# How far instructions may run ahead, set for each stage, and 24 columns of layer 1's first expert table in whole fp32

## The chip, the cores and the metric

The kernel runs on one core of a Trainium2 chip. The metric is the time of one execution on the device in microseconds (us), the median over several executions. PE is TensorE (matrix products), DVE VectorE, ACT ScalarE, POOL GpSimd, SP SyncE, which here issues most of the DMAs.

## The reference

Two layers of a diffusion block over 256 latent rows `x` and 256 context rows `ctx`, each 1024 wide. Each layer has a token mixer (differential attention, windowed attention and a gated delta rule, merged by gates) and a feed-forward part that looks up experts:

```python
def peer_ffn(h, wq, keys, u_tab, v_tab):            # cut
    q = (t @ wq).reshape(n, PEER_HEADS, 2, PEER_HALF)          # 8 heads
    s = jnp.einsum('thcd,cnd->thcn', q, keys)                  # 2 x 128 keys
    sv, si = lax.top_k(s, PEER_TOPK)                           # 16 of 128
    ...
    cv, ci = lax.top_k(cand, PEER_TOPK)                        # 16 of 256 sums
    eid = (i1 * N_KEYS + i2).reshape(n, PEER_HEADS * PEER_TOPK)
    gw = jax.nn.softmax(cv, axis=-1)
    act = gelu(einsum('pd,ped->pe', tb, u_tab[eb]))
    return einsum('pe,ped->pd', act * gb, v_tab[eb])

for l in range(DEPTH):                               # DEPTH = 2
    ...
    m, mc = token_mixer(h, hc, ...)                  # mc only in layer 0
    x = x + gt1 * m
    x = x + gt2 * peer_ffn(modulate(x, ...), ...)
    if need_ctx:                                     # layer 0
        xc = xc + gt1c * mc
        xc = xc + gt2c * peer_ffn(modulate(xc, ...), ...)
```

All of it is fp32. The output is `x` after layer 1.

## The kernel before

**Stages.** In order of the program: the context mixer of layer 0, the context's route of experts, the latent mixer of layer 0, the dense expert part of layer 0, the context mixer of layer 1, the latent mixer of layer 1, the dense expert part of layer 1. The context's experts of layer 0 are done in another way than the latent ones: `peer_gather` fetches the rows that were chosen out of both tables (U0, V0 for one half of the 256 rows, U1, V1 for the other) with indirect DMAs, one DVE instruction ("gather dot") for each fetched row of the first table, and small PE products for the second. This work is a lane of its own that runs beside the latent mixer and the dense part of layer 0, and its sum `acc` is stored to memory and read again by `add_peer` at the start of layer 1.

**The dense part** (`peer_dense`) multiplies all 16384 experts: the first table is taken as 128 columns of 128 experts (`first`, label "dU"), then Gelu, then the product with the weights of the route, then the second table (label "dV"). A column of the first table is 512 KB. It is multiplied in one of two ways. *Split:* ACT rounds the column to fp32r (the high part), DVE subtracts that from the column (the low part), and `mm3` multiplies high by high, high by low and low by high: 3 x 8 products of 128x256. *Whole:* 8 products in fp32 of the column and a third copy `full` of the normed rows that `norm_T` then keeps. In layer 0 columns 0 to 31 (`U4`) are whole, in layer 1 none. The route (`route`, eight heads, each: projection with `wq` split by DVE and ACT, scores, top 16 twice) and the building of the weight tables (`weights`, labels "didx" and "build") have a higher priority (`RBASE`) than the columns, which fill gaps; `pre` columns (32 in layer 0, 64 in layer 1) may be multiplied ahead of the second table.

**The order.** No engine's order is written by hand. `Rec.add` records every operation, and `Rec.order` plans all of them as a list scheduler with costs of its own; it gives out tiles of four sizes (`b4`, `b2`, `b1` in SBUF, `ps` in PSUM). An operation that takes a new tile out of the program's order is asked for its distance: the work, in us of the planner's own costs, between it and the first operation of its lane that isn't planned yet. `blocked` refuses it beyond `FAR` = 80; beyond `NEAR` = 20 it must leave some tiles of each size free (`SPARE`). One exception: in the context mixer of layer 1 (`FREE1`), once the gather lane is done, there is no limit to the distance, with other numbers of tiles left free (`FREE`). All instructions of the program are issued from one line of `emit` (L627 before, L624 after), so the profile's rows are told apart by tiles and shapes: `b` is any working tile, `ps` PSUM, `rows` and `ga` the gather's, `psv`, `pcd`, `pii`, `pgw` the route's.

Of the kernel before, what the change touches and what calls it, by code (L numbers as in the profile page):

```python
# [39 lines left out]
NC = sum(ni * nj for _, ni, nj in CAND)  # L40
LEVELS = (1, 2, 4, 8, 16, 32, 64)
WN = 32
U4, V4 = range(32), ()
WPOOL = ()
UP0, UP1 = (), ()
PRE1 = 64
# [5 lines left out]

ACTB = (1, 1)
GBASE, RBASE = 0, -8000
TAIL, FREE1 = 0, True
FREE = {"b4": 4, "b2": 2, "b1": 1, "ps": 0}
PRE = 32
LOAD = {"tensor": 1.0, "vector": 0.3, "scalar": 0.2}
NEAR, FAR, URGENT = 20.0, 80.0, 0.0

WHOLE = range(16)
LOADS = 0
# [207 lines left out]

class Op:
    __slots__ = ("i", "eng", "meth", "args", "kw", "dur", "dma", "preds", "succ", "tiles", "prio",
                 "npred", "ready", "lab", "lane", "cw", "port", "free")


NAMES = []
# [10 lines left out]
class Rec:  # L287
# [5 lines left out]
    def __init__(self, nc, pools, bufs):  # L293
        self.nc, self.pools, self.bufs = nc, pools, bufs
        self.ops, self.tiles = [], []
        self.tensor, self.vector = Eng(self, "tensor"), Eng(self, "vector")
        self.scalar, self.gpsimd, self.sync = Eng(self, "scalar"), Eng(self, "gpsimd"), Eng(self, "sync")
        self.base = 0
        self.lane, self.cw, self.free = 0, {}, False
        self.lab = ""  # L300
        self.why, self.prevt, self.inslot, self.fin = {}, {}, {}, {}

# [46 lines left out]
    def add(self, eng, meth, args, kw):  # L349
        o = Op()  # L350
# [34 lines left out]
                    t.acc = [a for a in t.acc if not ((a[3] | reg) == reg and pr[0] <= a[2][0] and a[2][1] <= pr[1])]  # L385
            t.acc.append((o.i, wr, pr, reg))
        o.preds = list(preds)
        o.lane, o.free = self.lane, self.free
        o.cw = self.cw[o.lane] = self.cw.get(o.lane, 0.0) + o.dur * LOAD.get(eng, 0.0) * (URGENT if self.base == RBASE else 1.0)
        o.prio = self.base + o.i  # L390
        o.succ = []
# [12 lines left out]
    def order(self):  # L404
# [89 lines left out]
        def blocked(o):  # L494
            for t in o.tiles:
                if t.kind == "dr" or t in live:
                    continue
                if not slots[t.tag] and not borrow(t.tag):
                    return t.tag
                f = first[t]  # L500
                lane = owner[t.tag]
                front = ops_at(lane)
                if f > front:
                    keep = 0
                    if o.lane >= 0:
                        head = ops[lanes[o.lane][lpos[o.lane]]]
                        dist = o.cw - head.cw
                        free = o.free and lpos[-1] >= len(lanes[-1]) - TAIL
                        if dist > FAR and not free:
                            return "far"  # L510
                        if free and dist > NEAR:
                            keep = FREE.get(t.tag, 0)
                        elif dist > NEAR or o.lane != main:
                            keep = SPARE.get(t.tag, 0) + (LOADS if o.dma and t.tag == "b4" else 0)
                    if load[t.tag][front:f].max() + 1 > cap[t.tag] - keep:
                        return t.tag
            return None
# [113 lines left out]
class Kern:  # L631
# [1138 lines left out]
        return newS, self.out_proj(mT, xt, l, pr, s)  # L1770

    def run(self):
        self.setup()
        self.silu_c()
        pr, pr1 = self.layer_cols(0), self.layer_cols(1)
        self.layer_rows(0, pr)
        self.ada(0, pr, 0, 8)
        kv = self.kv_tiles()
        hT = self.norm1(self.I["ctx"], pr, 1)
        fill = [lambda n=n: self.ada(1, pr1, n, n + 1, 2) for n in range(24)]  # L1780
        if ADA1 == 3:
            self.fill = fill
        S, oTs = self.main(0, 1, hT, pr, kv, None, True)
        self.ada(0, pr, 8, 24)
        mT = self.merge(hT, 0, pr, oTs)
        xc, xs = self.out_proj(mT, self.I["ctx"], 0, pr, 1)
        self.dump("xc0", xc)
        F = self.peer_front(0, 1, xs, pr)
        self.wpool = WPOOL
        if ADA1 == 4:  # L1790
            self.fill = fill
        self.whole = True
        _, (x, xs) = self.mix(0, 0, self.I["x"], pr, kv, S)
        self.whole = False
        self.dump("x0", x)
        self.layer_rows(1, pr1)
        self.nc.lane, self.nc.base = -1, GBASE
        acc = self.peer_gather(0, 1, F)
        self.nc.lane, self.nc.base = 0, 0

        def extra(c0):
            if ADA1 == 2 and c0 % 4 == 0 and c0 >= 32:
                self.ada(1, pr1, c0 // 4 - 8, c0 // 4 - 7, 2)
        x = self.peer_dense(0, 0, x, xs, pr, u4=U4, v4=V4, extra=extra, pre=PRE, up=UP0)
        self.dump("x1", x)
        self.wpool = ()
        pass
        self.lab("1 norm1")
        self.nc.free = FREE1
        xs = self.add_peer(1, xc, acc, pr)  # L1810
        hT = self.norm_T(xs, pr1["A1"][:, :, 1], pr1["mod"][:, 0:8, 1])
        kv = self.kv_tiles()
        S, _ = self.main(1, 1, hT, pr1, kv, None, False)
        self.nc.free = False
        _, (x, xs) = self.mix(1, 0, x, pr1, kv, S)
        self.dump("x2", x)
        self.peer_dense(1, 0, x, xs, pr1, self.out, pre=PRE1, up=UP1)


def body(tc, I, out, dbg=None):  # L1820
# [22 lines left out]
```

## Time and profile before

| | |
|---|---|
| median of three runs | 3811.16 us (3800.89 to 3819.09) |
| the profiled execution, its own time | 3817.58 us |
| its span in the profile | 3815.8 us |
| PE busy | 3463.5 us |
| DVE, ACT, POOL busy | 2374.0, 1707.0, 818.8 us |
| layer 1's dense part | 2866 to 3813 us |

The span is the time between the first and the last recorded instruction. Busy times are shares of that span; times of single instructions are given from its start.

### The profile page before, as it was taken

What the parts mean: (1) busy time and instruction counts of PE and PEld (TensorE: products, weight loads), DVE (VectorE), ACT (ScalarE), POOL (GpSimd) and SP (SyncE); (2) the same over time, 40 slices, a digit from 0 to 9 for tenths busy, and PEclk for the clock granted to TensorE, in tenths of its full rate; (3) what the DMA queues carried; (4) which work ended last, traced back from release to release, by engine and by line L of the source; (5) the groups of instructions that cost most, each with busy time, mean ns of one, the idle gap of its engine ahead of it and who ended that gap; (6) DMA issues with size and microseconds to landing.
All of it is one profiled execution on the core that took longest, in us unless ns stands there. A gap on an engine that the chain in (4) does not pass through costs nothing.

```text
span 3815.8 us, 62556 instructions
## 1 busy us (share of the span) xinstructions
PE 3463.5 (91%) x23800; PEld 2960.3 (78%) x23800; DVE 2374.0 (62%) x5288; ACT 1707.0 (45%) x3554; POOL 818.8 (21%) x716
## 2 busy tenths in 40 slices
PE   8999994987998987999999999998995789999999
PEld 6875993876797674788777778887795679889998
DVE  4542569887556783988544455645568963665554
ACT  4743441541543181343333347763543564444443
POOL 1010001476123434655444311101010000000000
PEclk9996997988899998999999998989997899999999
DMA  6346753597277889999899961212262364776562
GB/s 256 117 138 223 239 191 127 181 332 274 75 254 276 292 291 394 409 372 365 337 359 338 342 250 40 84 45 94 62 233 72 119 185 150 243 280 227 199 211 105
DMA packets 300956, 837.67 MB, mean 220 GB/s; under 512 B 26736, under 2 KB 96752, under 8 KB 300656
## 3 DMA queue, kind: packets, MB, share of 16 engines
q1 hardware_dynamic: 153168, 522.80, 38.6%
q0 software_dynamic: 73728, 268.47, 18.9%
q10 hardware_dynamic: 73760, 42.40, 3.7%
q8 instruction: 188, 3.08, 0.3%
q14 instruction: 112, 0.92, 0.1%
HBM read 792.67 MB, written 40.89 MB: 218 GB/s over the span
## 4 chain that ended last, share of the span: by engine, by line
PE 49%; DVE 4%; ACT 3%; issue 1%; DMA 1%; ACTq 0%; POOL 0%; POOLq 0%; DVEq 0%
PE ps L627 49%; ACT b L627 3%; DVE b L627 3%; DVE psi L627 0%; DVE psv L627 0%; ACTq L627 0%; DMA gd<-b 0%; DMA b<-in_v_tab 0%; DMA b<-in_u_cols 0%; DVE pii L627 0%; DVE pS L627 0%; DVE pci L627 0%; DVE dst L627 0%; DVE ga L627 0%; POOL qrs L627 0%
## 5 line engine op out<-in xcount | busy, mean ns | idle before, releaser
L627 PE MATMUL ps<-b,b 128*128 128x256 f32 (+4 forms) x18016 | 2761.0, 314 | 194.5 <-DVE b L627 121.6
L627 PEld LDWEIGHTS ps<-b,b 128*128 128x128 f32 (+1 forms) x18016 | 2452.5, 192 | 489.8 <-DVE b L627 141.9
L627 DVE TENSOR_TENSOR b<-b,b 128x1024 fp32r<-128x1024 f32 (+3 forms) x1218 | 1137.0, 977 | 718.5 <-ACT b L627 509.1
L627 ACT CAST b<-b 128x1024 fp32r<-128x1024 f32 (+1 forms) x918 | 850.2, 972 | 481.3 <-PE ps L627 341.0
L627 ACT COPY b<-ps 128x256 f32<-128x256 f32 (+3 forms) x896 | 289.2, 350 | 492.6 <-PE ps L627 483.5
L627 POOL DMA_INDIRECT rows<-in_u_tab,eid x256 | 349.4, 1365 | 321.5 <-DVE rows L627 232.7
L627 ACT ACTIVATE b<-ps 128x512 f32<-128x512 f32 (+1 forms) x266 | 137.5, 520 | 619.5 <-PE ps L627 609.6
L627 POOL DMA_INDIRECT rows<-in_v_tab,eidT x256 | 290.6, 1135 | 502.4 <-PE ps L627 442.4
L627 DVE SCALAR_TENSOR_TENSOR rows<-rows,ga 128x1024 f32<-128x1024 f32 x256 | 306.1, 1224 | 58.2 <-DMA rows<-in_u_tab,eid 58.2
L627 PE MATMUL ps<-consts,b 128*128 128x128 f32 (+1 forms) x1290 | 251.5, 312 | 84.1 <-DVE b L627 64.9
L627 PE MATMUL ps<-b 128*128 128x128 f32 (+1 forms) x2048 | 272.9, 301 | 37.8 <-ACT b L627 36.7
L627 PEld LDWEIGHTS ps<-b 128*128 128x128 f32 (+1 forms) x2048 | 231.6, 203 | 81.8 <-ACT b L627 60.0
L627 PEld LDWEIGHTS ps<-consts,b 128*128 128x128 f32 x1290 | 181.6, 179 | 131.9 <-issue 50.2
L627 DVE COPY_PREDICATED b<-masks,ps 128x64 f32<-128x64 uint8 (+1 forms) x416 | 83.2, 252 | 132.4 <-PE ps L627 129.4
L627 PE MATMUL ps<-rows,ga 128*32 128x512 f32 x1024 | 139.2, 599 | 7.2 <-DMA rows<-in_v_tab,eidT 7.2
L627 ACT COPY b<-b 128x128 f32<-128x128 f32 x384 | 108.0, 305 | 44.7 <-DVE b L627 42.3
L627 POOL TENSOR_TENSOR b<-b,b 128x512 f32<-128x512 f32 x24 | 45.5, 1896 | 351.7 <-DVE b L627 326.2
L627 DVE TENSOR_SCALAR b<-consts,b 128x128 f32<-128x128 f32 x384 | 110.3, 346 | 0.0
L627 DVE TENSOR_TENSOR b<-ps,b 128x128 f32<-128x128 f32 (+4 forms) x144 | 61.9, 455 | 72.3 <-PE ps L627 48.6
L627 DVE TENSOR_TENSOR b<-consts,b 128x512 f32<-128x512 f32 x128 | 87.0, 685 | 13.5 <-DMA gd<-b 8.6
L627 PE MATMUL ps<-b,cs 128*32 128x256 f32 x768 | 76.5, 460 | 11.6 <-DVE cs L627 11.6
L627 PEld LDWEIGHTS ps<-rows,ga 128*32 128x32 f32 x1024 | 29.2, 109 | 73.3 <-issue 45.0
(176 smaller groups left out, 1567.5 us busy)
## 6 DMA issues: line engine op xcount, KB each, us to landing
b<-in_u_cols SPq DMA_DIRECT2D x256, 512.0 KB, 5.5
b<-in_v_tab SPq DMA_DIRECT2D x256, 512.0 KB, 6.5
b<-in_w_in SPq DMA_DIRECT2D x184, 512.0 KB, 6.5
gd<-b ACTq DMA_DIRECT2D x64, 512.0 KB, 5.2
b<-gd SPq DMA_DIRECT2D x64, 512.0 KB, 5.7
b<-in_w_ada SPq DMA_DIRECT2D x48, 512.0 KB, 8.2
b<-in_w_ada SPq DMA_DIRECT2D x96, 256.0 KB, 4.6
b<-in_wq SPq DMA_DIRECT2D x48, 512.0 KB, 6.1
```

The costliest lines, as they stand in the source:

```text
L627: r = getattr(getattr(nc, o.eng), o.meth)(*[_real(x) for x in o.args], **{k: _real(x) for k, x in o.kw.items()})
```

## The change

Two parts. The limit of the distance is no longer one number: each operation carries the limit `far` of its stage, from the six numbers of `FARS`: 250 for the setup, the context mixer of layer 0 and its route, 150 for the latent mixers, 200 for the dense parts, 80 for the context mixer of layer 1. The exception in the context mixer of layer 1 is gone. And columns 0 to 23 of layer 1's first table are multiplied whole (`U41`); `norm_T` keeps `full` there too, in two tiles of size `b4`.

```diff
-U4, V4 = range(32), ()
+U4, U41, V4 = range(32), range(24), ()
...
-TAIL, FREE1 = 0, True
-FREE = {"b4": 4, "b2": 2, "b1": 1, "ps": 0}
...
-NEAR, FAR, URGENT = 20.0, 80.0, 0.0
+NEAR, URGENT = 20.0, 0.0
+
+FARS = (250, 150, 200, 80, 150, 200)
...
-        o.lane, o.free = self.lane, self.free
+        o.lane, o.far = self.lane, self.far
...
                         dist = o.cw - head.cw
-                        free = o.free and lpos[-1] >= len(lanes[-1]) - TAIL
-                        if dist > FAR and not free:
+                        if dist > o.far:
                             return "far"
-                        if free and dist > NEAR:
-                            keep = FREE.get(t.tag, 0)
-                        elif dist > NEAR or o.lane != main:
+                        if dist > NEAR or o.lane != main:
                             keep = SPARE.get(t.tag, 0) + (LOADS if o.dma and t.tag == "b4" else 0)
...
     def run(self):
+        self.nc.far = FARS[0]
         self.setup()
...
+        self.nc.far = FARS[1]
         self.whole = True
         _, (x, xs) = self.mix(0, 0, self.I["x"], pr, kv, S)
...
+        self.nc.far = FARS[2]
         self.nc.lane, self.nc.base = -1, GBASE
         acc = self.peer_gather(0, 1, F)
...
         self.lab("1 norm1")
-        self.nc.free = FREE1
+        self.nc.far = FARS[3]
         xs = self.add_peer(1, xc, acc, pr)
...
-        self.nc.free = False
+        self.nc.far = FARS[4]
         _, (x, xs) = self.mix(1, 0, x, pr1, kv, S)
         self.dump("x2", x)
-        self.peer_dense(1, 0, x, xs, pr1, self.out, pre=PRE1, up=UP1)
+        self.nc.far = FARS[5]
+        self.peer_dense(1, 0, x, xs, pr1, self.out, u4=U41, pre=PRE1, up=UP1)
```

The program has 384 fewer PE products (576 of the split kind less, 192 whole ones more), 24 fewer DVE and 24 fewer ACT instructions; the DMAs are the same in number and size.

**PE, layer 1's route, around the eighth head.** Before: `ps_28549` and `ps_28569` are the scores of the seventh head, `ps_28565` is the projection of the eighth, and the rows between are the first products of four split columns (`b_5436`, `b_5437` are high and low parts of the normed rows).

```order
L627 MATMUL ps_28549<-b_5448_27145,b_5576_28468 128x128 x4
L627 MATMUL ps_28565<-b_5436_27953,b_5619_28102 128x256
L627 MATMUL ps_28565<-b_5437_27974,b_5619_28102 128x256
L627 MATMUL ps_28569<-b_5448_27145,b_5607_28556 128x128 x4
L627 MATMUL ps_28579<-b_5436_27953,b_5819_28168 128x256
L627 MATMUL ps_28579<-b_5437_27974,b_5819_28168 128x256
L627 MATMUL ps_28583<-b_5436_27953,b_5827_28212 128x256
L627 MATMUL ps_28583<-b_5437_27974,b_5827_28212 128x256
L627 MATMUL ps_28590<-b_5436_27953,b_5834_28259 128x256
L627 MATMUL ps_28590<-b_5437_27974,b_5834_28259 128x256
L627 MATMUL ps_28594<-b_5436_27953,b_5842_28305 128x256
L627 MATMUL ps_28594<-b_5437_27974,b_5842_28305 128x256
```

The next row is the projection of the eighth head again. After, at the same place (`ps_28568` is the seventh head's last scores, `ps_28564` the eighth head's projection, `b_5430` and `b_5431` are the whole normed rows):

```order
L624 MATMUL ps_28564<-b_5438_27953,b_5617_28145 128x256
L624 MATMUL ps_28564<-b_5439_27962,b_5617_28145 128x256
L624 MATMUL ps_28568<-b_5446_26129,b_5605_28555 128x128 x4
L624 MATMUL ps_27951<-b_5431_27964,b_5816_27824 128x256 x4
L624 MATMUL ps_27951<-b_5430_27937,b_5817_27911 128x256 x4
L624 MATMUL ps_27951<-b_5431_27964,b_5817_27911 128x256 x4
...
L624 MATMUL ps_28954<-b_5430_27937,b_5842_28527 128x256 x4
L624 MATMUL ps_28954<-b_5431_27964,b_5842_28527 128x256 x4
L624 MATMUL ps_28564<-b_5438_27953,b_5618_28986 128x256
```

In all 31 rows of four, 124 whole products, now stand between the seventh head's scores and the eighth head's projection, where 8 split ones stood.

**PE, the end of the context's route in layer 0.** Before: `ps_6829` is the route's last scores, `ps_7029` the transposes of the expert ids; `ps_6869`, `ps_6938` and `ps_6983` are whole products of the latent stream's delta-rule projections (`b_1409`, `b_1410` its normed rows).

```order
L627 MATMUL ps_6829<-b_1201_5103,b_1381_6815 128x128 x4
L627 MATMUL ps_6837<-consts_71,b_1412_6118 128x128 x4
L627 MATMUL ps_6847<-consts_71,b_1412_6118 128x128 x4
...
L627 MATMUL ps_6869<-b_1409_6822,b_1467_6327 128x256 x4
L627 MATMUL ps_6869<-b_1410_6872,b_1468_6329 128x256 x4
...
L627 MATMUL ps_6983<-b_1409_6822,b_1484_6794 128x256 x4
L627 MATMUL ps_6983<-b_1410_6872,b_1485_6797 128x256 x4
L627 MATMUL ps_7029<-consts_71,b_1404_6997 128x128 x2
```

After, from the last scores (`ps_6802`) to the transposes of the ids (`ps_6963`):

```order
L624 MATMUL ps_6802<-b_1201_3293,b_1381_6788 128x128 x4
L624 MATMUL ps_6791<-consts_71,b_1411_5675 128x128 x2
L624 MATMUL ps_6796<-consts_71,b_1411_5675 128x128 x2
L624 MATMUL ps_6818<-consts_71,b_1412_5688 128x128 x2
L624 MATMUL ps_6825<-consts_71,b_1412_5688 128x128 x2
L624 MATMUL ps_6832<-b_1409_6823,b_1467_5743 128x256 x2
L624 MATMUL ps_6844<-b_1409_6823,b_1475_6024 128x256 x4
L624 MATMUL ps_6860<-b_1428_6762,b_1419_6836 128x256
L624 MATMUL ps_6832<-b_1409_6823,b_1467_5743 128x256 x2
L624 MATMUL ps_6886<-b_1419_6836,w_abh_5379 16x256
L624 MATMUL ps_6963<-consts_71,b_1404_6959 128x128 x2
```

Of those projections 8 products are left between the two, where 48 stood; the rest comes later in the row. On DVE, 13 gather dots stand inside the route where 5 stood.

**PE, the boundary of the layers.** The last gather products (`rows`, `ga`) stood 221 rows ahead of the first norm transposes of layer 1, among split products of the dense part. After, they stand 81 rows ahead of them, and this follows them:

```order
L624 MATMUL ps_17306<-rows_20835,ga_18197 32x512
L624 MATMUL ps_17306<-rows_20847,ga_18197 32x512
L624 MATMUL ps_14532<-b_4119_20888,b_4117_20976 128x512
L624 MATMUL ps_14532<-b_4122_20907,b_4116_20969 128x512
L624 MATMUL ps_14532<-b_4123_20927,b_4116_20969 128x512
```

These are products of the second table's last columns; before, columns of the first table stood there too.

## Rows read from the trace of the kernel before

**Rows 1.** Head of the page: span, busy time, share and instructions of each engine.
```profile
span 3815.8 us, 62556 instructions
...
PE 3463.5 (91%) x23800; PEld 2960.3 (78%) x23800; DVE 2374.0 (62%) x5288; ACT 1707.0 (45%) x3554; POOL 818.8 (21%) x716
```

**Rows 2.** Busy time of each engine in nine stretches (us from the start).
```profile
core 0: us, PE busy (x) PEld busy (x) DVE busy (x) ACT busy (x) POOL busy (x), PEclk, DMA share, GB/s
2921.00:2967.00 46.00, 0.45 (x5) 0.25 (x3) 45.18 (x241) 0.06 (x1) 0.00 (x0) 0.53 0.00 0
2967.00:3003.00 36.00, 29.89 (x228) 29.07 (x228) 27.62 (x85) 14.27 (x25) 0.00 (x0) 0.88 0.33 118
3003.00:3107.00 104.00, 77.56 (x539) 70.21 (x540) 90.68 (x257) 80.71 (x250) 0.00 (x0) 0.93 0.57 164
3107.00:3807.00 700.00, 700.00 (x4419) 632.51 (x4419) 371.77 (x438) 312.24 (x370) 0.00 (x0) 1.00 0.59 202
3150.00:3200.00 50.00, 50.00 (x423) 50.00 (x422) 20.80 (x18) 21.07 (x27) 0.00 (x0) 1.00 0.45 142
2878.00:2996.00 118.00, 72.27 (x594) 71.82 (x592) 104.95 (x505) 28.89 (x38) 0.00 (x0) 0.80 0.23 77
653.00:676.00 23.00, 22.58 (x109) 19.15 (x108) 22.55 (x87) 7.39 (x16) 1.75 (x2) 1.00 0.31 116
700.00:960.00 260.00, 214.91 (x1291) 177.25 (x1290) 219.16 (x505) 98.79 (x348) 181.89 (x156) 0.84 0.81 286
1181.00:1322.00 141.00, 137.83 (x905) 105.48 (x904) 110.04 (x517) 27.58 (x37) 56.51 (x56) 1.00 0.79 283
```

**Rows 3.** Timeline of PE, layer 0's whole columns (start, us, count).
```profile
1250.91 10.63 PE L627 MATMUL ps<-b,b 128*128 128x256 f32 x48
...
1264.06 7.17 PE L627 MATMUL ps<-b,b 128*128 128x256 f32 x32
```

**Rows 4.** Groups of instructions by form: busy us, mean ns, idle before.
```profile
L627 DVE TENSOR_TENSOR b<-b,b 128x1024 fp32r<-128x1024 f32 x754 | 914.7, 1245 | 331.3 <-ACT b L627 188.4 <-PE ps L627 72.0 <-issue 50.0
L627 ACT CAST b<-b 128x1024 fp32r<-128x1024 f32 x754 | 763.3, 1048 | 379.4 <-PE ps L627 320.1 <-DVE b L627 29.5 <-POOL b L627 11.0
...
L627 DVE SCALAR_TENSOR_TENSOR rows<-rows,ga 128x1024 f32<-128x1024 f32 x256 | 306.1, 1224 | 58.2 <-DMA rows<-in_u_tab,eid 58.2
```

**Rows 5.** Timeline of PE, layer 1's route; in brackets the idle time before.
```profile
2966.93 28.66 PE L627 MATMUL ps<-b,b 128*128 128x256 f32 x222 [45.55 <-DVE b L627]
```

**Rows 6.** Timeline of DVE, the same place.
```profile
2965.68 10.29 DVE L627 TENSOR_TENSOR b<-b,b 128x1024 fp32r<-128x1024 f32 x9
2981.76 0.87 DVE L627 MAX8 psv<-b 128x8 f32<-128x128 f32 x4 [5.80 <-ACT b L627]
...
3001.55 1.28 DVE L627 TENSOR_TENSOR b<-consts,b 128x512 f32<-128x512 f32 x2
```

**Rows 7.** Timeline of PE, the context's route in layer 0.
```profile
608.84 6.19 PE L627 MATMUL ps<-b,b 128*128 128x256 f32 x34 [34.08 <-DVE b L627]
...
642.10 8.01 PE L627 MATMUL ps<-b,b 128*128 128x256 f32 x46 [17.91 <-DVE b L627]
...
656.50 18.42 PE L627 MATMUL ps<-b,b 128*128 128x256 f32 x84 [0.42 <-ACT b L627]
```

**Rows 8.** Timeline of PE, the boundary of the layers.
```profile
2220.01 1.92 PE L627 MATMUL ps<-rows,ga 128*32 128x512 f32 x16
2221.87 28.30 PE L627 MATMUL ps<-b,b 128*128 128x256 f32 x192
...
2254.10 5.90 PE L627 MATMUL ps<-b,b 128*128 128x512 f32 x24 [0.35 <-ACT b L627]
2266.98 3.64 PE L627 MATMUL ps<-consts,b 128*128 128x128 f32 x16 [6.98 <-issue]
```

**Rows 9.** Timeline of SP's DMA issues, the same place.
```profile
2222.70 0.33 SPq L627 DMA_DIRECT2D xd<-ga  x1
2230.63 1.91 SPq L627 DMA_DIRECT2D b<-xd  x4
```

**Rows 10.** Timeline of DVE, the first and the last sums there.
```profile
2252.89 0.69 DVE L627 TENSOR_TENSOR b<-ps,b 128x512 f32<-128x512 f32 x1 [0.44 <-PE ps L627]
...
2261.32 0.69 DVE L627 TENSOR_TENSOR b<-b,b 128x512 f32<-128x512 f32 x1
```

**Rows 11.** DMA issues from 2220 to 2262: count, KB each, median us to landing.
```profile
b<-xd SPq DMA_DIRECT2D x4, 512.0 KB, 5.6
```

More of the change, by code (lines that the diff above doesn't have):

```diff
@@ L272 @@
     __slots__ = ("i", "eng", "meth", "args", "kw", "dur", "dma", "preds", "succ", "tiles", "prio",
-                 "npred", "ready", "lab", "lane", "cw", "port", "free")
+                 "npred", "ready", "lab", "lane", "cw", "port", "far")
 NAMES = []
@@ L298, in __init__ @@
         self.base = 0
-        self.lane, self.cw, self.free = 0, {}, False
+        self.lane, self.cw, self.far = 0, {}, 0.0
         self.lab = ""
```

## The prediction

> **What bounds the kernel now.** I read the head of the page first: PE is busy for 3463.5 of 3815.8 us, 91%, while DVE has 62% and ACT 45% [rows 1]. The product engine is therefore the one to watch, and the next view is the table of stretches, which shows where it is not the bound [rows 2]. In layer 1's dense stage it falls into three kinds. From 2921 to 2967 PE works 0.45 us of 46 while DVE works 45.18: the route of the experts (top 16 of eight heads) is bound by DVE. From 3003 to 3107, where the weight tables are built, DVE has 90.7 and ACT 80.7 of 104 us. From 3107 to the end PE has 700.00 of 700 us, DVE 372 and ACT 312. So each us of PE work that leaves the last stretch leaves the time, and work that PE does inside the 46 us hole is free, unless it delays the route itself.
>
> **The changed part with the largest price: layer 1's columns.** A split column takes 24 products of 128x256, a whole column 8 products in fp32, each recorded as two. Between 3150 and 3200 PE runs 423 records in 50 us, 0.118 each [rows 2]; I round up to 0.119, which moves the sum by 0.4 us, and a split column is 24 x 0.119 = 2.85 us. Layer 0 has whole columns already: 48 records take 10.63 us and 32 take 7.17, so 16 records are 3.46 us, 0.432 for one whole product [rows 3]. By work alone the edit costs 24 x (3.46 - 2.85) = +14.4 us.
> The Trainium skill, "FP8 and Floating Point Precision", section on TensorE precision, says that true fp32 makes four passes through the array. Against three split products that would be 4/3 x 2.85 = 3.80 us for a column and +22.9 us in all; the trace's 3.46 us, which is shorter, is what the sum goes by.
> It also removes 24 DVE subtractions (1245 ns each) and 24 ACT casts (1048 ns), 29.9 and 25.2 us [rows 4]. They lie beside a PE that is never idle, in a stretch where DVE is used for 53% and ACT for 45% [rows 2], so I price them at nothing; their cover is PE's 700 us. The column loads stay the same.
>
> **Where those products stand.** What a column costs matters less than when it runs. In the order before, 176 of the split products stand ahead of the first weight-building product: 8 before the eighth head's projection, 46 between it and its scores, 122 after. In the order after, all 192 whole ones and two split ones do: 4 ahead of the heads, 124 in one run between the seventh head's scores and the eighth head's projection, 16 ahead of its scores, 48 behind them. None stands in the building stretch in either. A whole column has no DVE subtraction to wait for, so the DVE-bound route no longer holds it back. What is left for the bound stretch is 2896 x 0.119 = 344.6 us before and (2496 - 2) x 0.119 = 296.8 after: **-47.7 us**.
> The 124 are 53.6 us of PE work in a hole of 45.55 us, and the eighth head's projection stands behind them. Before, it began at 2966.93 [rows 5], as soon as DVE began its split at 2965.68 [rows 6]. PE now begins the 124 at about 2922 and gets to that head at 2975.5. Projection (5.5), 16 whole products (6.9) and scores (1.1) take it to about 2989, and DVE's last top 16, which began at 2981.76 after 5.80 us of waiting [rows 6], begins at 2989.6. Then 32 whole products (13.8 us) and 16 more (6.9) stand ahead of the transposes of the ids, while DVE needs 19.8 us from its last top 16 to the building (2981.76 to 3001.55). So building starts near 3010.5: **+9**. The least is 0 (PE clears the run as DVE gets there). The most is 24: layer 0's route, which has this mix of whole products under it, took 141 us with PE busy for 137.8 [rows 2]; layer 1's takes 118 (2878 to 2996).
>
> **The distances.** The rest of the diff changes no count, only order, in the stages ahead.
> *Context route's end, layer 0.* Before, 48 whole products of the latent stream stand between the last scores and the transposes of the ids, as rows of 84 records, 18.42 us [rows 7]; PE is busy 22.6 of the 23 us from 653 to 676, and DVE 22.6 too [rows 2]. After, 8 do. So 40 x 0.432 = 17.3 us of PE work move out from under a DVE-bound stretch to a later place; and 13 instead of 5 gather dots of 1224 ns [rows 4] stand inside it, 9.8 us of DVE work. Against that the dots leave the stretch 700 to 960, where DVE has 219 of 260 us and PE 215 [rows 2], so PE gets part of it back. Bounds 0 and 27; I take a third, **+9**.
> *Layer boundary.* Before, the last gather product on PE ends at 2221.9, and some 38 us of PE work are behind it, so the accumulated rows' store (2222.70), load (2230.63) and landing (5.6 us after the issue's end, about 2238) are long done when PE's last products let DVE's sums begin at 2252.9 [rows 8 to 11]. Even so PE idles 6.98 us ahead of the norm's transposes at 2266.98 [rows 8]. After, 81 rows instead of 221 stand between the two, some 16 us of work. The same 16.2 us from the last gather product to the landing now end when PE runs dry, at about 2260; the eight sums of the dense stage and then the eight of the gather, 0.69 us each [rows 10], go to about 2272.6, and the transposes begin at 2274.5: **+7.5**, from 0 (the landing is hidden in what order PE gives) to 15 (PE also loses the 7 it had). What is late next is the context mixer of layer 1, whose first products wait for those transposes.
> *All else.* By the two orders, priced with the rows above, the delta-rule chains of the context mixers end some 14 (layer 0) and 31 us of PE work (layer 1) earlier in PE's order, and attention fills in behind them; but PE's total is unchanged, and in the orders of the latent mixers and of layer 0's dense stage I find nearly the same rows. I take **-6**, bounds -12 and +6: the 6.98 us of idle [rows 8] is the scale of one such hole.
>
> **Sum.** -47.7 + 9 + 9 + 7.5 - 6 = -28.2 us. The profiled execution took 3817.6 us, so 3789.4; it is 6.4 above the median of the three timed runs, 3811.2, and against that the forecast is **3783 us**. With all bounds low the change is -59.7 (3751), with all high +24 (3835).
>
> **Rivals.**
> *B, the moves cost nothing:* the context route and the boundary are covered, only part of the route's slip stays; -42 to -59, 3752 to 3769. For it: PE had an idle hole of 17.91 us just ahead of the route's end [rows 7]. Against it: DVE has no slack there.
> *C, nearly all is given back:* the route of layer 1 stretches to layer 0's 141 us, or the context stage loses its 27; a sum of -15 to +5, 3796 to 3816. For it: the eighth head waits behind 124 products in one run, and nothing on PE may pass them.
> *D, the other side, slower:* the clock. PEclk is 0.53 in the hole from 2921 to 2967, near the lower level of 1.2 GHz, and 0.88 right after it [rows 2], since PE has nothing to do there. If the 188 whole products that now stand there were run at half speed throughout, they would cost 188 x 0.432 = 81 us more: +53, 3864. It decides once more than 28.2/81 = 35% of them run low. Against it: in layer 0's route, with the same products under it, the granted clock was 1.00 [rows 2], since PE was busy; a full PE should hold it here too.
> The Trainium skill, "TensorE: Matmul & The Clock Gate", says that an idle TensorE drops to 1.2 GHz; the 0.53 above agrees, and so a filled hole should do the opposite of D.
> *E, more holes are filled:* the idle 34.08 and 17.91 us in the context's route [rows 7] too; -60 or more, below 3751. In the order no product moves into them.
> That the change doesn't do what it says (tiles, not the distance, hold the columns back) is excluded by the order: the block has moved.
>
> **How the numbers follow.** Forecast (-15 to -42) 0.48, B 0.15, C 0.25, D 0.05, E 0.04, several bounds at their high end at once 0.03. The range 3755 to 3815 takes the forecast, nearly all of B and nearly all of C. 0.5% is 19 us, about what the three runs, 18 us apart, can tell from no change: faster is below 3792, slower above 3830. Faster: 0.85 of the forecast, B and E, 0.60. Same: the rest of the forecast, C and a little of the last, 0.33. Slower: 0.07.
>
> **What would show it.** In the profile after: the idle 45.55 us ahead of the eighth head becomes a run of about 248 records at 0.216 us with PEclk near 1; the building starts 0 to 24 us later, counted from the end of the dense norm; the fully busy stretch is some 48 us shorter than 700. PE's wait ahead of layer 1's first transposes is 10 to 16 us. From 653 to the end of the context's route PE has idle time. Wrong would be: a building that starts over 30 us later than before, counted from the dense norm; whole products of over 0.5 us there; or a latent mixer of a layer that is over 12 us longer or shorter, of which the orders show me no cause.

## The result and the profile after

The changed kernel takes 3776.85 us, the median of seven runs (3761.3 to 3789.25), against 3811.16 (3800.89 to 3829.84) of the kernel before: ratio 0.9899, 95% interval 0.987 to 0.9927, some 38 us less by the ratio and 34 by the medians. The forecast was 3783. The profiled execution of the changed kernel took 3761.3 us, the fastest of the seven, so its span of 3759.5 is 15 us better than the typical one.

The head of its page, which answers to [rows 1]:

```profile
span 3759.5 us, 62220 instructions
...
PE 3445.1 (92%) x23608; PEld 2944.4 (78%) x23608; DVE 2346.9 (62%) x5264; ACT 1690.5 (45%) x3530; POOL 820.6 (22%) x716
```

The table of stretches of the changed kernel, the same columns as [rows 2]: the route of layer 1, the middle of the run of whole products in it, the building of the weight tables, the end stretch.

```profile
2863.00:2982.00 119.00, 119.00 (x729) 110.24 (x728) 92.50 (x494) 23.28 (x34) 0.00 (x0) 1.00 0.41 138
...
2915.00:2955.00 40.00, 40.00 (x187) 35.22 (x186) 34.48 (x181) 3.24 (x6) 0.00 (x0) 1.00 0.34 106
...
2992.00:3098.00 106.00, 79.32 (x538) 70.44 (x539) 89.30 (x256) 81.93 (x247) 0.00 (x0) 0.94 0.61 175
3098.00:3750.00 652.00, 650.38 (x4013) 583.32 (x4012) 352.82 (x422) 292.43 (x345) 0.00 (x0) 1.00 0.59 204
```

The hole is gone: PE is busy for all 119 us of the route, at a granted clock of 1.00, and 187 records in 40 us are 0.214 us each, 0.428 for a whole product (forecast from [rows 3]: 0.432). The end stretch is 652 us long rather than 700.

Timelines of the changed kernel, first PE (from the dense norm's transposes on), then DVE at the eighth head, which answer to [rows 5] and [rows 6]:

```profile
2849.83 3.68 PE L624 MATMUL ps<-consts,b 128*128 128x128 f32 x16 [7.51 <-DVE b L624]
...
2854.58 128.52 PE L624 MATMUL ps<-b,b 128*128 128x256 f32 x797
2982.94 0.38 PE L624 MATMUL ps<-consts,pii 128*128 128x128 f32 x2
...
3093.12 7.80 PE L624 MATMUL ps<-b,b 128*128 128x256 f32 x48 [7.00 <-ACT b L624]
3102.54 47.67 PE L624 MATMUL ps<-b,b 128*128 128x256 f32 x399 [1.62 <-ACT b L624]
```

```profile
2969.94 0.87 DVE L624 MAX8 psv<-b 128x8 f32<-128x128 f32 x4 [19.96 <-ACT b L624]
...
2990.89 0.69 DVE L624 TENSOR_TENSOR b<-consts,b 128x512 f32<-128x512 f32 x1 [1.49 <-ACT b L624]
```

In the kernel before the same transposes stood here:

```profile
2869.59 3.46 PE L627 MATMUL ps<-consts,b 128*128 128x128 f32 x16 [7.09 <-DVE b L627]
```

They are the zero from which the route is counted: they end at 2873.0 before and 2853.5 after. DVE's last top 16 starts 108.7 us behind that before ([rows 6]) and 116.4 after, the building 128.5 and 137.4. So the route is 8.9 us longer, forecast +9, and DVE now waits 19.96 us rather than 5.80 for the eighth head's scores, which stand behind the run of 124 products. New is the stop at the end of the building, 7.00 and 1.62 us, where before PE had stopped for 3 us (the kernel before):

```profile
3105.91 24.31 PE L627 MATMUL ps<-b,b 128*128 128x256 f32 x181 [3.03 <-DVE b L627]
```

Timeline of PE at the boundary of the layers, which answers to [rows 8]:

```profile
2220.89 1.92 PE L624 MATMUL ps<-rows,ga 128*32 128x512 f32 x16
2222.74 6.89 PE L624 MATMUL ps<-b,b 128*128 128x512 f32 x52
...
2255.89 3.65 PE L624 MATMUL ps<-consts,b 128*128 128x128 f32 x16 [17.10 <-issue]
```

PE idles 17.10 us there rather than 6.98: +10.1, forecast +7.5. The third place of the forecast, the end of the context's route in layer 0, in the same view (to [rows 7]):

```profile
657.30 1.76 PE L624 MATMUL ps<-consts,b 128*128 128x128 f32 x6 [17.93 <-DVE b L624]
```

PE waits 17.93 us there for the transposes of the ids. The lengths of the stages, from PE's first and last record of each, worked out from each trace (context mixer of layer 0, its route, latent mixer, dense part with the boundary, both mixers of layer 1, layer 1's dense part to the end):

```
                     ctx L0   route  lat L0  dense L0  mixers L1  dense L1    span
before                527.2   147.9   483.4    1108.4      595.5     953.3  3815.8
after                 502.8   155.2   485.9    1112.0      586.4     917.2  3759.5
before, again         528.6   147.9   483.6    1117.4      603.8     951.8  3833.1
after, again          506.5   156.0   508.0    1112.2      586.2     917.3  3786.2
whole columns only    526.8   147.7   483.5    1117.6      603.8     929.0  3808.2
whole only, again     521.3   147.8   483.1    1118.9      595.5     929.8  3796.5
distances only        505.0   155.5   492.7    1112.2      586.3     957.1  3808.8
36 whole columns      502.2   155.6   519.4    1113.2      594.9     893.1  3778.3
48 whole columns      512.8   154.7   492.4    1112.6      586.1     890.1  3748.7
first distance 80     529.0   154.9   508.3    1112.2      587.7     917.9  3809.9
second distance 80    505.6   137.6   474.4    1142.2      594.5     918.4  3772.8
80 x5, 200            527.5   147.9   487.1    1116.8      581.3     916.4  3777.0
80 x5, 200; 40 col.   530.3   147.9   484.5    1115.3      578.6     884.5  3741.1
250, 80 x4, 200; 40   513.3   137.6   479.7    1135.7      590.5     885.0  3741.8
```

The last column is one execution and moves by up to 27 us between two of one kernel (after and after, again); most stages repeat within 1 to 9 us. So the stages are compared, and the timed ratios decide on the whole.

### The profile page after: what moved, and what is told of

It reads as the page before. It is cut to its first block, busy times and chain, and to the rows that moved or that the text cites. A ratio compares the mean times of both kernels' runs of the same rounds, so it can differ in the third digit from the quotient of the medians.

```text
span 3759.5 us, 62220 instructions
## 1 busy us (share of the span) xinstructions
PE 3445.1 (92%) x23608; PEld 2944.4 (78%) x23608; DVE 2346.9 (62%) x5264; ACT 1690.5 (45%) x3530; POOL 820.6 (22%) x716
## 4 chain that ended last, share of the span: by engine, by line
PE 52%; ACT 3%; DVE 2%; DMA 2%; issue 1%; ACTq 0%; POOL 0%; POOLq 0%; SPq 0%; DVEq 0%
PE ps L624 52%; ACT b L624 3%; DVE b L624 2%; DMA gd<-b 1%; ACTq L624 0%; DMA b<-in_u_cols 0%; DVE rows L624 0%; DMA b<-in_v_tab 0%; POOL qrs L624 0%; DVE dst L624 0%; DVE gS L624 0%; DVE qrs L624 0%; ACT L624 0%; POOL hrs L624 0%; POOLq L1840 0%
## 5 line engine op out<-in xcount | busy, mean ns | idle before, releaser
L624 PE MATMUL ps<-b,b 128*128 128x256 f32 (+5 forms) x17824 | 2756.9, 315 | 146.0 <-DVE b L624 72.9
L624 PEld LDWEIGHTS ps<-b,b 128*128 128x128 f32 (+2 forms) x17824 | 2445.1, 191 | 446.1 <-DVE b L624 91.8
L624 DVE TENSOR_TENSOR b<-b,b 128x1024 fp32r<-128x1024 f32 (+3 forms) x1194 | 1106.0, 968 | 709.3 <-ACT b L624 507.9
L624 ACT CAST b<-b 128x1024 fp32r<-128x1024 f32 (+1 forms) x894 | 826.7, 969 | 529.6 <-PE ps L624 340.3
L624 ACT ACTIVATE b<-ps 128x512 f32<-128x512 f32 (+1 forms) x266 | 137.4, 520 | 693.2 <-PE ps L624 649.3
L624 POOL TENSOR_SCALAR qrs<-qrs 128x8 f32<-128x8 f32 (+1 forms) x24 | 14.1, 588 | 331.0 <-DVE qrs L624 300.1
```

Source lines behind the costliest of these rows:

```text
L624: r = getattr(getattr(nc, o.eng), o.meth)(*[_real(x) for x in o.args], **{k: _real(x) for k, x in o.kw.items()})
```

## The experiments

**The whole columns alone, and the distances alone.** Two kernels take one part each.

```diff
 # whole columns only: the kernel before with
-U4, V4 = range(32), ()
+U4, U41, V4 = range(32), range(24), ()
...
-        self.peer_dense(1, 0, x, xs, pr1, self.out, pre=PRE1, up=UP1)
+        self.peer_dense(1, 0, x, xs, pr1, self.out, u4=U41, pre=PRE1, up=UP1)
 # distances only: the changed kernel with
-U4, U41, V4 = range(32), range(24), ()
+U4, U41, V4 = range(32), (), ()
```

> The distances of the kernel before (80, and the exception in layer 1's context mixer), with the 24 whole columns alone. The order has 184 whole products ahead of the building of the weight tables, against 192 in the changed kernel. Theory of the prediction (a whole column runs in the route's hole since it waits for no DVE subtraction; the distance has no part in it): the 46 us hole ahead of the eighth head is filled, building starts some 8 to 11 us later counted from the end of the dense norm, the fully busy stretch behind it loses 344.6 - 2496 x 0.119 = 47.6 us; sum -36 to -40, ratio 0.990. Rival (the columns need the longer distance to get there): most of the hole stays, 0 to -10, ratio 0.997 to 1.000.

Measured: 3799.97 us, ratio 0.9942 (0.9913 to 0.9971), between both theories. Layer 1's dense part is 929.0 us, 24.3 shorter than before and 11.8 longer than in the changed kernel. The hole is filled; what is lost lies at the end of the building. Timeline of PE, ACT and SP's DMA issues in that kernel (q behind the engine: DMA issues):

```profile
3126.63 2.08 PE L627 MATMUL ps<-b 128*128 128x128 f32 x8 [6.35 <-ACT b L627]
...
3142.65 0.80 PE L627 MATMUL ps<-b,b 128*128 128x256 f32 x2 [9.10 <-ACT b L627]
```

```profile
3110.58 1.25 ACTq L627 DMA_DIRECT2D gd<-b  x2
...
3117.62 8.21 ACTq L627 DMA_DIRECT2D gd<-b  x2
3125.93 2.31 ACT L627 COPY b<-ps 128x256 f32<-128x256 f32 x8 [8.06 <-issue]
...
3134.49 7.02 ACTq L627 DMA_DIRECT2D gd<-b  x2
```

```profile
3114.18 32.62 SPq L627 DMA_DIRECT2D b<-in_u_cols  x19
```

ACT issues the stores of the weight tables itself. As soon as SP issues 19 column loads in a burst, two pairs of these issues take 8.21 and 7.02 us from the start of the first to the end of the second, rather than 1.25; ACT's copies wait behind them, and PE waits 6.35 and 9.10 us for ACT. The first pair is long because the issues are: 3.20 and 4.79 us. The second pair is 0.59 and 2.14 us of issuing, and between the two ACT waits 4.2 us for an earlier store to land. The stores land late too. The DMA issues of that kernel, first from 3034 to 3106, then from 3114 to 3142 (count, KB each, median us to landing):

```profile
gd<-b ACTq DMA_DIRECT2D x22, 512.0 KB, 4.4
```

```profile
gd<-b ACTq DMA_DIRECT2D x8, 512.0 KB, 14.2
```

> The six distances of the changed kernel, no whole column in layer 1. Theory of the prediction: the route of layer 1 keeps its idle 45 us; only the terms +9 (context route), +7.5 (boundary) and -6 (all else) are left, +10, ratio 1.003 (bounds -12 and +48). Rival (the distances pay in the context mixer of layer 0, which ended 24 us earlier in the profile of the changed kernel at a higher granted clock from 240 to 360): -10 to -25, ratio 0.993 to 0.997, and PEclk near 0.9 from 240 to 360 again.

Measured: 3814.05 us, ratio 1.000 (0.9977 to 1.0023). The route keeps its hole:

```profile
2958.01 17.25 PE L624 MATMUL ps<-b,b 128*128 128x256 f32 x124 [43.97 <-DVE b L624]
```

So alone the six distances are worth nothing that can be measured, and yet they move stages both ways: the context mixer of layer 0 is 22 us shorter, its route 8 and the latent mixer 9 longer, the mixers of layer 1 are 9 shorter. Neither sum is met (1.003, and 0.993 to 0.997), and each holds for a part.

**More columns.** The changed kernel with `U41 = range(48)` and `range(36)`.

> The changed kernel with 48 whole columns rather than 24. The order has 208 whole products ahead of the building and 64 more inside it. Theory of the prediction (what counts is what is left for the fully busy end stretch): 112 x 0.432 + 1920 x 0.119 = 276.9 us left rather than 296.8, -20; building ends 7 to 12 us later, since 64 x 0.432 = 27.6 us go into a stretch in which PE has 26 of 104 us free, and 16 more products stand ahead of it: -8 to -13 against the changed kernel, ratio to the kernel before 0.987. Rival (a whole column is only more work, 0.6 us each, once the hole is full): +5 to +14 against the changed kernel, ratio 0.991 to 0.994.

Measured: 3751.39 us, ratio 0.9842 (0.9812 to 0.9873), some 22 us less than the changed kernel (0.0057 of 3811), more than the theory's 8 to 13. Layer 1's dense part is 890.1 us rather than 917.2, and at the end of its building PE has no stop at all, with the same burst of loads (busy for 30 of 30 us, DMA share 1.05):

```profile
3090.00:3120.00 30.00, 30.00 (x179) 27.44 (x178) 5.03 (x16) 10.46 (x32) 0.00 (x0) 1.00 1.05 357
```

The whole columns that stand behind the building need nothing of ACT or DVE ahead of their products and cover the 8.6 us stop.

> The changed kernel with 36 whole columns. As with 48, the order has 272 whole products (34 columns) up to the end of the building. Theory (a whole column pays where PE has room and costs 0.61 us each where it has none): 12 columns go back to split in the full stretch, -7 us against 48 columns, ratio to the kernel before 0.982. Rival (whole columns behind the building cover the burst of loads there, which the split ones wait for: with 24 PE idled 8.6 us there, with 48 none): the hole opens again, 0 to +3 against 48, ratio 0.984 to 0.985.

Measured: 3768.39 us, ratio 0.985 (0.9826 to 0.9873), and 893.1 us for the stage. The times alone don't part 36 columns from 48, since the intervals overlap; the stage and its stop do. The rival held: the stop is back, and it eats the 7 us of saved products.

```profile
3146.94 0.79 PE L624 MATMUL ps<-b,b 128*128 128x256 f32 x2 [8.65 <-ACT b L624]
```

Here ACT's cast stands behind a DMA issue that is itself only 1.39 us long, but begins at 3143.92, when an earlier transfer of ACT's queue has landed. So it is the wait for a landing and not a long issue that makes this stop.

**The last distance.**

```diff
-FARS = (250, 150, 200, 80, 150, 200)
+FARS = (80, 80, 80, 80, 80, 200)
```

> All distances 80 but the last, which is 200, the exception in layer 1's context mixer gone, 24 whole columns: against the run with whole columns alone only the distance in layer 1's dense stage differs there (192 whole products and 4 split ones ahead of the building, against 184). Theory (what the run with whole columns alone lost is the burst of 19 column loads at the end of the building, beside which two pairs of DMA issues of ACT took 8.2 and 7.0 us and PE idled 6.35 and 9.10; a longer distance starts those loads earlier): PE's idle there is under 10 us as in the changed kernel, sum -34 to -40, ratio 0.990. Rival (the distance in this stage does nothing, since the columns ahead of the building are nearly the same): idle of 12 to 16 us there again, ratio 0.994.

Measured: 3787.69 us, ratio 0.9906 (0.9886 to 0.9925). The stage takes 916.4 us, as in the changed kernel (917.2) and 13 less than with the whole columns at distance 80; one stop of 6.91 us is left, beside 11 loads rather than 19. The last distance does have a part, and it goes with the start of the column loads, since the products ahead are nearly as many: of the loads, 33 are issued more than 10 us ahead of the building's end (before 3095) rather than 23 (with the whole columns at distance 80, before 3110). The DMA issues from 2800 on, first with the whole columns at distance 80, then with the last distance at 200:

```profile
b<-in_u_cols SPq DMA_DIRECT2D x23, 512.0 KB, 4.9
```

```profile
b<-in_u_cols SPq DMA_DIRECT2D x33, 512.0 KB
```

> The run with whole columns alone once more, for a second profile: its 12 times lie in two groups, 3767 to 3784 and 3796 to 3810. If the stop at the end of the building (15.5 us of PE idle) is what parts them, an execution of the first group shows less than 8 us there and one of the second group 12 us or more; if the clock of the earlier stages parts them, the stop is the same in both.

Measured: 3798.24 us, an execution of the second group, with stops of 8.94 and 6.93 us, together as long as in the first profile. The stop belongs to the order. No execution of the first group was profiled, but the granted clock, the mean over a whole execution, is on record for each of the 12: 0.946 to 0.952 in the four of the first group, 0.938 to 0.943 in the eight of the second. So the groups go with the clock, which the second theory has; in which stage it differs is not shown.

**The first distances.** First the kernel before, then one distance set back.

> The kernel before, profiled once more, to see what of the difference in the context mixer of layer 0 belongs to the order and what to the single execution. If the low granted clock from 240 to 360 (0.66) belongs to the order, it is between 0.6 and 0.75 again and that mixer's last output product ends near 529 us; if to the execution, it lies elsewhere or is gone, and the mixer ends 10 to 25 us from there.

Measured: 3834.95 us; the mixer ends at 528.6, and from 300 to 360 PE shows what it showed the first time. The table of stretches from 300 to 360: the kernel before, then before again, then the changed kernel.

```profile
300.00:360.00 60.00, 57.80 (x220) 35.13 (x221) 16.69 (x54) 19.46 (x62) 1.23 (x2) 0.50 0.41 140
```

```profile
300.00:360.00 60.00, 56.38 (x210) 34.60 (x214) 17.35 (x57) 19.83 (x63) 1.23 (x2) 0.50 0.41 142
```

```profile
300.00:360.00 60.00, 56.92 (x517) 40.80 (x516) 25.57 (x86) 30.11 (x91) 3.06 (x4) 0.94 0.64 227
```

In the old order PE is busy for 94 to 96% of these 60 us and runs them at the lower level of its clock (0.50), so that it gets 210 to 220 records done; in the new one, equally busy, it gets 517 done at 0.94. By the timeline the old stretch holds products of the attention with 64 rows or 64 columns, small transposes and the 32-column products of the modulation. The new stretch holds all of these kinds too, with more products of the modulation (232 records rather than 64) and 49 records of full 128x256 products, of which the old one has none. What of this holds the clock up is not shown: no run changed one kind alone.

> The changed kernel with the first of its six distances, that of the setup, the context mixer of layer 0 and its route, set back from 250 to 80; everything else as changed. Three profiles with the old order of that mixer ended its output products at 527 to 529 us, three with the new one at 503 to 513. Theory now (in the old order its attention products run in one block at a granted clock of 0.50 from 300 to 360; the longer distance mixes them with other products): the mixer ends near 527 again with PEclk 0.50 from 300 to 360, some 20 us come back, ratio 0.995. Rival (those profiles differ by chance, or the time is made up in the next stage): ratio 0.990 as in the changed kernel.

Measured: 3827.78 us, ratio 1.0007 (0.9977 to 1.0038): more than either theory gives. The context mixer ends at 529.0 with PEclk 0.50 from 300 to 360, as expected. But the loss against the changed kernel, 41 us, is larger than these 20 to 26; the profiled execution adds 508.3 us in the latent mixer of layer 0. The twelve executions lie from 3797 to 3852 us, and the times go with the mean granted clock, from 0.948 in the shortest to 0.928 in the longest; the seven of the changed kernel have 0.944 to 0.955.

> The changed kernel profiled again, for the spread of its stages between executions. Theory (the order fixes the context mixer of layer 0 at 503 to 513 us and layer 1's dense part at 917; the latent mixer of layer 0 varies with the granted clock, 486 to 519 us so far with this order against 483.1 to 483.6 with the old one): the same three ranges again. Rival (the changed kernel's 486 belongs to its order): latent mixer within 3 us of 486.

Measured: 3788.01 us. Context mixer 506.5, layer 1's dense part 917.3, as the theory has it; the latent mixer takes 508.0, so the 485.9 of the first profile was no property of the order. With this mixer's new order six profiles show 485.9 to 519.4 us, mean 501; with the old one four show 483.1 to 483.6. The table of stretches for this mixer: the kernel before, then the changed kernel, changed again, and 36 whole columns, whose order of this mixer is the same.

```profile
675.00:1159.00 484.00, 434.33 (x2904) 373.30 (x2906) 354.26 (x735) 209.32 (x545) 216.89 (x187) 0.89 0.65 228
```

```profile
658.00:1144.00 486.00, 457.87 (x3055) 386.29 (x3059) 352.80 (x732) 216.03 (x556) 232.62 (x196) 0.93 0.69 238
```

```profile
662.00:1170.00 508.00, 475.56 (x3050) 396.46 (x3051) 353.17 (x733) 216.93 (x557) 228.80 (x196) 0.89 0.66 228
```

```profile
657.80:1177.20 519.40, 489.49 (x3055) 408.81 (x3059) 352.96 (x731) 216.93 (x556) 229.84 (x196) 0.86 0.65 223
```

The six go with the granted clock of the mixer: 485.9 us at 0.93, 492.4 and 492.7 at 0.91, 508.0 and 508.3 at 0.89, 519.4 at 0.86. But the clock is not all of it. At the same 0.89 the new order takes 508 us and the old one 484: PE has some 150 records more there and is busy 41 us longer. By the counts of the stages these come in about equal parts out of the route and out of the dense part, which hold as many fewer. What the first distance gains (20 us) the second gives back on the mean (7 in the route, 18 in this mixer).

> The changed kernel with the second of its six distances, that of layer 0's latent mixer, set back from 150 to 80. The order has 48 latent projections under the end of the context's route again, as before (8 in the changed kernel), and the last gather products behind the second table's last product. Theory (the distance of 150 gives back in the route and in this mixer what the 250 ahead of it gains): the route takes 126 to 137 us rather than 142, the latent mixer 480 to 487 rather than 486 to 519, 20 to 30 us less than the changed kernel, ratio 0.982 to 0.985. Rival (the gain of the best run came from the distances of 150 and 200 further on, or the latent mixer's spread comes with the early context mixer): ratio 0.988 to 0.991, and the mixer over 490 us.

Measured: 3764.7 us, ratio 0.9878 (0.9836 to 0.9919); against the changed kernel's 0.9899 that is no difference. Yet route and latent mixer are about as short as the theory says or shorter, 137.6 and 474.4 us, and 29 us or more are gained by there. They are lost at the boundary, where this order has the last gather products behind everything else of layer 0. Timeline of PE:

```profile
2202.56 1.05 PE L624 MATMUL ps<-consts,modT 128*128 128x128 f32 x8
2203.54 1.92 PE L624 MATMUL ps<-rows,ga 128*32 128x512 f32 x16
...
2241.59 1.90 PE L624 MATMUL ps<-rows,ga 128*32 128x512 f32 x10 [0.23 <-DMA rows<-in_v_tab,eidT]
2259.85 2.40 PE L624 MATMUL ps<-consts,b 128*128 128x128 f32 x10 [16.36 <-DVE b L624]
```

From 2203 PE has only the gather left, row by row as its DMAs land, until 2243. PE's own work of layer 0 ends 36 us earlier than in the changed kernel (2202.7 against 2238.8), and layer 1 starts 4 us later (2259.9 against 2255.9): here the gather's lane bounds it, not PE.

**The best of both.** The distances ahead of the last one at 80, or at 250 for the first alone, with 40 whole columns:

```diff
-U4, U41, V4 = range(32), range(24), ()
+U4, U41, V4 = range(32), range(40), ()
...
-FARS = (250, 150, 200, 80, 150, 200)
+FARS = (80, 80, 80, 80, 80, 200)      # and (250, 80, 80, 80, 80, 200)
```

> The five distances ahead of layer 1's dense part at 80, the exception gone, the last distance 200, and 40 whole columns. Theory (the columns are worth what they leave to the full end stretch, and the five or six columns behind the 34 that fit ahead cover the burst of loads there; the other distances are worth nothing together): layer 1's dense part from the last output product of its mixer takes 885 to 890 us, the run with the same distances and 24 columns took 916; so -28 against that run, -64 against the kernel before, ratio 0.983, and no stop of over 4 us at the end of the building. Rival (that stretch has a limit of its own near 890 to 893 whatever the columns): ratio 0.984 to 0.985.

Measured: 3747.96 us, ratio 0.9816 (0.978 to 0.9852). The stage takes 884.5 us and has no stop of over 0.7 us at its building's end: that is what the theory of the columns expected (885 to 890).

> As the run beside it with 40 whole columns, but the first distance at 250. In its order the last gather products stand behind the last product of layer 0's second table, 0 us of PE work ahead of its end (15.8 in the changed kernel, 37.4 in the kernel before). Theory of the prediction for the boundary (from the last gather product to the landing of its sums takes 16 us, and what PE has left beside it is the cover): PE idles 30 to 35 us ahead of layer 1's first transposes, against 17.1 and 7.0; the context mixer of layer 0 ends near 505 rather than 527, and both nearly cancel: 0 to +5 against the run beside it. Rival (the boundary is bound by the sums on DVE, wherever the last gather product stands): idle of 17 to 20 us, -10 to -15 against the run beside it.

Measured: 3725.07 us, ratio 0.9744 (0.9714 to 0.9773), 23 us less than the run beside it and the best of all. Neither theory has that time. The timeline of PE at the boundary, then the same place in the run beside it:

```profile
2222.45 2.35 PE L624 MATMUL ps<-rows,ga 128*32 128x512 f32 x16
2225.54 1.05 PE L624 MATMUL ps<-rows,ga 128*32 128x512 f32 x2 [0.73 <-DMA rows<-in_v_tab,eidT]
...
2246.79 1.90 PE L624 MATMUL ps<-rows,ga 128*32 128x512 f32 x10 [0.20 <-DMA rows<-in_v_tab,eidT]
2266.35 3.68 PE L624 MATMUL ps<-consts,b 128*128 128x128 f32 x16 [17.66 <-DVE b L624]
```

```profile
2277.98 3.65 PE L624 MATMUL ps<-consts,b 128*128 128x128 f32 x16 [9.52 <-issue]
```

The wait ahead of the transposes is 17.66 us, as the rival has it, and not 30 to 35. But it is not all that PE loses there. From 2224.8 to 2248.7 PE has only the gather left, as in the run before: 64 records, which at the rate of a full row of 16 (1.92 us) would be 7.7 us of work, take 23.9. By this estimate 16 us go there, and with the wait 34, which is what the theory of the prediction gave for the whole; the stage with the boundary is 20 us longer than in the run beside it. In the changed kernel 17.1 us pass from the end of the second table's products to the transposes, here as many from the end of the gather's, and 16.4 in the run with the second distance set back: that the later of the two ends counts fits these three.

What pays is ahead of the boundary: the context mixer of layer 0 is 17 us shorter, its route 10, the latent mixer 5. The two profiled executions took the same time, 3743.57 and 3742.86 us, and that of this run is the longest of its six; the other five have a mean granted clock of 0.951 to 0.957, those of the run beside it 0.940 to 0.951. So the 23 us of the timed runs go with the clock, and no profile shows in which stage.

## Why the prediction was right, point by point

**Layer 1's columns, -47.7.** Right in its mechanism. From the building's end (PE's last building product) to the last product of the second table it is 705.6 us before and 663.4 after, and the building itself is 2.5 us shorter: -44.7. What is missing is the stop of 8.6 us rather than 3 at the building's end, +5.6, which the prediction didn't have. That the distance has no part in it, as the nearly equal counts in the order (184 and 192) suggested ahead of the run with whole columns alone, was wrong: with distance 80 the stop is 15.5 us, 7 of the 12 us by which the stage is longer there.

**The route's slip, +9.** Measured +8.9, in the way described: the eighth head behind 124 products.

**fp32's price.** 0.428 us a product in the hole and 0.432 in [rows 3]. The Trainium skill's four passes ("FP8 and Floating Point Precision", section on TensorE precision) would make 4 x 0.119 = 0.476 of it, as an estimate; the traces of both kernels are below that. Whether the rule is off here or the 0.119 as the price of one pass, which a split product takes from start to start, no run shows.

**Context route, +9.** Measured +6.8 to +8.3 in the six profiles that have the new order there. But the work that moves out of the route is not given back behind it, as the term had it: at an equal granted clock the latent mixer is some 25 us longer (508 against 484), with part of that work in it. With the 7 of the route that is 32 us, beyond the term's bound of 27; the dense part, with 72 records less, takes some of it back.

**Boundary, +7.5.** +10.1 of idle time, a wait of 17.1 us where the prediction named 10 to 16; but counted as a stage, from the end of the latent mixer to those transposes, the new order is no longer than the old one (1112 against 1108 to 1119): the dense part ahead of it is shorter by as much.

**All else, -6, bounds -12 and +6.** This term failed in what it is made of. The context mixer of layer 0 gives -20 (old 521 to 530, new 502 to 513), through the granted clock (the same 3951 or 3952 records of PE in both orders, busy for 494 us before and 470 after), of which the prediction had no step; the latent mixer costs +2 to +36, where it found "nearly the same rows"; the mixers of layer 1 give -12 on the mean (old 595 to 604, new 586 to 595). A latent mixer over 12 us longer was one of the prediction's own signs of being wrong, and three of the six profiles show it. In the sum these nearly cancel: the distances alone measured 1.000 with an interval of +-9 us, and the prediction's terms for them, +9 + 7.5 - 6, make +10, just beyond it. So the forecast of 3783 rests on a mechanism that was right, the columns', and on terms of the distances whose total came near by luck.

**Rivals.** D (the low clock in the hole) is refuted: 1.00 there. C asked for a route that is 23 us longer; it is 8.9 longer. B has 3752 to 3769 us: the fastest executions reach it, the median doesn't, and its reasons fail, since the route slipped by all of the 9 us and the boundary was not covered.

**Left open.** Why executions of one order differ in their granted clock, which moves the latent mixer of layer 0 between 486 and 519 us; and what in the old order of the context mixer keeps it at 0.50.

## What to carry to other kernels

Extra work on the bounding engine can pay when it removes a need of the engine that bounds elsewhere: a form of a product that costs 21% more, but waits for nobody, ran in a hole that the cheaper form could not enter. Count how much the hole holds, put that much there and a little more behind it as cover, and no more (layer 1's dense part: 917 us with 24 whole columns, 893 with 36, 885 with 40, 890 with 48). Give each stage's knob a run of its own: six distances that together measure 1.000 held one that is worth 23 us in other company and some that give it back. And when executions of one order differ, look at their granted clock first.

## What was not expected of the hardware

A PE that is busy for 94 to 97% of 60 us ran at a granted clock of 0.50 all the time, in six of seven profiles with that order (0.57 in the seventh, whose mixer ended 6 us earlier); with as much busy time the same stretch had 0.83 to 1.00 in the seven profiles of the other order, with 420 to 526 records rather than 205 to 222 (280 in the seventh).

A DMA issue on ACT's queue isn't free while another queue is bursting: a single issue mostly took 0.5 to 0.7 us, and up to 4.8 and 7.2 us beside 18 or 19 loads of 512 KB that SP issued (whole columns alone, both profiles). Its stores landed after 14.2 us there rather than 4.4, and part of what ACT lost was waiting for such a landing ahead of its next issue.
